# An empty step between the squares at a head's end and their column sums

## The chip, the cores and the metric

The kernel runs on one core of one Trainium2 chip. The metric is the device time of one execution in microseconds (us), and a version is told by the median of its runs. Before the change the median is 2241.21 us over three runs (2240.69 to 2246.49).

## The reference, cut to what matters

The reference is a two-layer trunk over 256 latent and 256 context tokens, 1024 channels wide, in float32. Each layer has three token mixers, merged by gates, and then a ConvFFN. Two of the mixers work in heads, eight each per layer, and both end a head with an RMS norm over its 128 channels:

```python
y_att = (rmsnorm(o, att_subln_g) * (1 - lam_init))      # differential attention
y_hg  = rmsnorm(o_f + flip(o_b), hg_norm_g) * silu(g)   # bidirectional HGRN2
rmsnorm(x, g) = x * rsqrt(mean(x * x, -1) + EPS) * g
```

The change moves nothing in the arithmetic. It concerns when, among other work, these two norms and all the steps ahead of them are issued. In layer 0 the heads produce all 512 tokens, in layer 1 the 256 latent ones only.

## The kernel before, in words

Layout. Activations lie with channels on the 128 partitions and tokens along the free axis. Each projection is three float32r matmul passes (high and low parts of weight and activation, `mm3`, lines 121 to 123); its weights come as float32 by DMA, ScalarE rounds them to the high part (line 111) and VectorE subtracts for the low part (line 112).

The heads stage. For each head h the kernel weaves three generators together: the projections that head h+1 needs (`project`, the main stream), the HGRN2 head h (`hg_head`) and the attention head h (`att_head`). `weave` (line 819) runs one step of the main stream, mostly 12 matmuls of 512 columns, then resumes the side generators up to their next `yield` where they are due. Side step i of c is due at `(i + 1) / (c + 1) * n * rate` main steps, where n is the number of main steps and c comes from the call:

```python
weave(main, n, m, (13, 2 * ns + 3), 0.92 if h + 1 < HEADS else (0.7, 0.85)[l])
```

So the counts are 13 for `hg_head`, and 11 (layer 0, ns = 4) or 7 (layer 1, ns = 2) for `att_head`. When the main stream has ended, what is left of the side generators runs to its end, `hg_head` first. A main stream has n = 12 steps in layer 0 and 9 in layer 1 where head h is even (below: a short head), and 8 more where h is odd (a long head: 20 and 17), because the values of two heads are projected at once. The last head of a layer is woven with `tail_proj` instead (n = 20 and 10, rates 0.7 and 0.85).

The order. TensorE's instructions stay in the order in which this Python code emits them. VectorE's, ScalarE's and GpSimd's are put in an order by a planner that works with its own costs: an instruction may be taken ahead of others that stand before it in the program, and work of head h+1 stands in VectorE's queue ahead of the end of head h. Each queue is then fixed and runs in order. PSUM has two sets of four banks: `pm` for the projections, `ps` for the heads.

The steps that this text speaks of, numbered by the `yield` that ends them:

- `hg_head`: H1 opens the head (gates, prefix sums, first level; no matmul). H2 sums the diagonal. H3 to H9 are six levels of masked products (matmuls at line 505, reading `K`, which VectorE makes in line 443 and GpSimd in line 445) with the neighbouring pairs among them. H10 makes the border products. H11 transposes the state keys (line 525) and ScalarE copies them out of PSUM (line 527). H12 multiplies them with the values (line 532), copied out in line 534. H13 accumulates the head's output `o` (lines 541 and 544) and takes the squares. What is behind the 13th `yield`, the column sums and the scaling, runs when the main stream has ended.
- `att_head`, layer 0 (layer 1): A1, A2 are the first scores (line 600); then transposes of the probabilities (line 617) and products with the values (line 624) alternate with further scores. A9 (A5) ends with the squares, A10 (A6) makes the column sums and scales, A11 (A7) is empty.

The norm itself: `rms_square` (line 312) has ScalarE square `o` (line 314) and round the squares to a high part (line 192), and VectorE make the low part (line 193); `rms_scale` (line 321) has TensorE sum both parts over the partitions with a matrix of ones (line 319), and ScalarE take the logarithm and the exponential (lines 325 and 326). The scaled head is stored to DRAM by SyncE's queue (line 942).

The scores of head h+1 need its queries and keys: `att_proj` ends each main stream of a short head with them, by a chain of VectorE (lines 575, 576, 581), GpSimd (line 577), ScalarE (line 582) and GpSimd again (line 583).

Of the kernel before, what the change touches and what calls it, by code (L numbers as in the profile page):

```python
# [21 lines left out]
HEADS = 8  # L22
# [25 lines left out]
def trunk(ctx: ExitStack, tc: tile.TileContext, A, out):  # L48
# [11 lines left out]
    @contextmanager  # L60
    def pool(name, side="left", **tags):
        with tc.tile_pool(name=name, bufs=1, side=side, reuse_waits="tile") as p:
            def get(tag, shape, dt=F32):
                return p.tile(shape, dt, tag=tag, name=tag, bufs=tags[tag])
            yield get
# [4 lines left out]
    def S(w):  # L70
        return sp.tile([P, w], F32, tag=f"s{w}", name=f"s{w}")
# [4 lines left out]
    def PS(shape):  # L76
        return psm.tile(shape, F32, tag="ps", name="ps")
# [22 lines left out]
    def pk(l, n):  # L100
        a, b = PK[n]
        return pack[l][:, a:b]
# [88 lines left out]
    def split(t, src):  # L191
        nc.scalar.copy(out=t[:, 0, :], in_=src)
        nc.vector.tensor_tensor(out=t[:, 1, :], in0=src, in1=t[:, 0, :].bitcast(F32), op=sub)  # L193
        return t
# [117 lines left out]
    def rms_square(get, o, n):  # L312
        sq = get("sq", [P, 512])
        nc.scalar.activation(out=sq[:, :n], in_=o, func=AF.Square)
        return sq, split(get("sqs", [P, 2, n], F32R), sq[:, :n])

    def column_sums(ps, parts):
        for i in range(2):
            nc.tensor.matmul(ps, lhsT=onesr, rhs=parts[:, 1 - i, :], start=(i == 0), stop=(i == 1))

    def rms_scale(sq, n):
        sq, parts = sq
        ms = PS([P, 512])
        column_sums(ms[:, :n], parts)
        nc.scalar.activation(out=sq[:, :n], in_=ms[:, :n], func=AF.Ln, scale=1.0 / P, bias=epsb)
        nc.scalar.activation(out=sq[:, :n], in_=sq[:, :n], func=AF.Exp, scale=-0.5)
        return sq
# [78 lines left out]
    def hg_head(get, l, h, z, k, q, gg, v, put, lbv, C0, NQ):  # L406
# [137 lines left out]
                    nc.tensor.matmul(o[:, c], lhsT=st[:, d, :], rhs=V[:, d, 0:T], start=False, stop=(d == 1))  # L544
        sq = rms_square(get, o, NQ)
        yield
        r = rms_scale(sq, NQ)
        nc.vector.scalar_tensor_tensor(out=r[:, :NQ], in0=o, scalar=pk(l, "hgn"), in1=r[:, :NQ], op0=mul, op1=mul)
        nc.vector.tensor_tensor(out=r[:, :NQ], in0=r[:, :NQ], in1=gg, op=mul)
# [36 lines left out]
    def att_head(get, l, qk, v, put, av, NQ):  # L586
        sc = 64 ** -0.5
        o = None

        def scores(qt):  # L590
            k0 = 0 if qt < 2 else 2
            nk = 4 - k0
            p = get("p", [P, 2, nk * P])
            mx = S(2)
            sm = S(2)
            pss = [PS([P, nk * P]) for _ in range(2)]
            for n, (a, b) in enumerate(((0, 1), (0, 0), (1, 0))):
                for i in range(2):
                    r = slice(64 * i, 64 * i + 64)
                    nc.tensor.matmul(pss[i], lhsT=qk[r, 0, a, qt * P:(qt + 1) * P], rhs=qk[r, 1, b, k0 * P:512],  # L600
                                     start=(n == 0), stop=(n == 2))
            for i in range(2):
                nc.vector.tensor_reduce(out=mx[:, i:i + 1], in_=pss[i], axis=AX.X, op=amax)  # L603
            nc.vector.tensor_scalar(out=mx, in0=mx, scalar1=-sc, scalar2=None, op0=mul)
            for i in range(2):
                nc.scalar.activation(out=p[:, i, :], in_=pss[i], func=AF.Exp, bias=mx[:, i:i + 1], scale=sc,
                                     accum_out=sm[:, i:i + 1])
            nc.vector.reciprocal(out=sm, in_=sm)
            nc.vector.tensor_tensor(out=sm[:, 1:2], in0=sm[:, 1:2], in1=av[:, 0:1], op=mul)
            nc.vector.tensor_scalar(out=p[:, 1, :], in0=p[:, 1, :], scalar1=sm[:, 1:2], scalar2=None, op0=mul)  # L610
            nc.vector.scalar_tensor_tensor(out=p[:, 0, :], in0=p[:, 0, :], scalar=sm[:, 0:1], in1=p[:, 1, :], op0=mul, op1=add)
            return p, k0, nk

        def turn(p, k0, nk):
            pt = PS([P, nk, P])
            for s in range(nk):
                nc.tensor.transpose(pt[:, s, :], p[:, 0, s * P:(s + 1) * P], ident)
            wt = get("wt", [P, nk, P])
            nc.scalar.copy(out=wt, in_=pt)
            return wt, k0, nk  # L620

        def values(qt, wt, k0, nk):
            for s in range(nk):
                nc.tensor.matmul(o[:, qt * P:(qt + 1) * P], lhsT=v[:, k0 + s, :], rhs=wt[:, s, :], start=(s == 0), stop=(s == nk - 1))

        n = NQ // P
        ps, ws = {}, {}
        for i in range(n + 2):
            if i < n:
                ps[i] = scores(i)  # L630
                yield
            if 2 <= i:
                if o is None:
                    o = PS([P, NQ])
                values(i - 2, *ws.pop(i - 2))
            if 1 <= i <= n:
                ws[i - 1] = turn(*ps.pop(i - 1))
                yield
        sq = rms_square(get, o, NQ)
        yield  # L640
        r = rms_scale(sq, NQ)
        nc.vector.scalar_tensor_tensor(out=r[:, :NQ], in0=o, scalar=av[:, 1:2], in1=r[:, :NQ], op0=mul, op1=mul)
        put(r[:, :NQ])
        yield
# [174 lines left out]
    def weave(main, n, sides, counts, rate):  # L819

        todo = sorted((((i + 1) / (c + 1) * n * rate, k) for k, c in enumerate(counts) for i in range(c)))
        done = 0
        end = object()
        while True:
            while todo and (todo[0][0] <= done or main is None):
                next(sides[todo.pop(0)[1]], None)
            if main is None:
                break
            if next(main, end) is end:
                main = None  # L830
            done += 1
        for g in sides:
            for _ in g:
                pass
# [100 lines left out]
    for l in range(DEPTH):  # L935
        ns = 4 if l == 0 else 2
# [4 lines left out]
        def putter(b, h):  # L941
            return lambda t: nc.sync.dma_start(out=ysp[b, h], in_=t)
# [23 lines left out]
        with pool("heads", lk=2, qg=1, qk=1, v=3, w=2, sq=2, sqs=2 if l else 1, wt=2, sc=1, E=6 if l else 4, K=2, p=2) as get, ExitStack() as even, \  # L966
                tc.issue_after(pre.ins):
            gete = even.enter_context(pool("even", lk=2, qg=1, qk=1, t=3, sh=2))
            gets = [lambda tag, *a: (gete if tag in ("lk", "qg", "qk", "t", "sh") else get)(tag, *a),
                    lambda tag, *a: (gete if tag in ("t", "sh") else get)(tag, *a)]  # L970

            def project(h, out, pss=None):
                if pss is not None:
                    yield from hg_proj(gets[h % 2], l, h, Xh, NQ, out, pss)
                if h % 2 == 0:
                    yield from v_proj(get, A["w_hi"][l, h // 2], Xh, out, "vh", whi if h == 0 else None)
                if pss is None:
                    yield from hg_proj(gets[h % 2], l, h, Xh, NQ, out)
                yield from att_proj(gets[h % 2], l, h, Xh, rope, NQ, out)
                if h % 2 == 0:  # L980
                    yield from v_proj(get, A["w_av"][l, h // 2], Xh, out, "va")

            def units(h):
                return (12 if l == 0 else 9) + (8 if h % 2 == 0 else 0)

            d = {}
            for _ in project(0, d, first):
                pass
            for h in range(HEADS):
                j = slice((h % 2) * P, (h % 2 + 1) * P)  # L990
                m = [hg_head(get, l, h, d["ls"], d["k"], d["qg"][:, 0, :], d["qg"][:, 1, :], d["vh"][:, :, j], putter(1, h),
                             lbv, (reset, masks), NQ),
                     att_head(get, l, d["qk"], d["va"][:, :, j], putter(0, h), attv[l], NQ)]
                if h + 1 < HEADS:
                    main, n = project(h + 1, d), units(h + 1)
                else:
                    even.close()
                    getv = rvt.enter_context(pool("vt", side="right", vt=ns))
                    vt = [getv("vt", [P, D]) for _ in range(ns)]
                    pus = []  # L1000
                    main, n = tail_proj(l, Xh, vt, ns, NQ, pus), 8 * ns // 2 + ns
                weave(main, n, m, (13, 2 * ns + 3), 0.92 if h + 1 < HEADS else (0.7, 0.85)[l])
        if l == 0:
            jobs += [(lambda get, scr, m=m: ada_row(get, scr, 0, m, 2)) for m in range(16, 48)]
        pre = nc.scalar.preload_act_table(AF.Gelu_apprx_tanh)
# [204 lines left out]
```

## Time and profile before

| | us |
|---|---|
| median of three runs | 2241.21 |
| the profiled execution | 2245.93 |
| its span, first to last instruction | 2244.2 |
| TensorE busy | 2128.5 (95%) |
| VectorE busy | 1727.2 (77%) |
| ScalarE busy | 1155.8 (52%) |

The span is what one profiled execution took from its first to its last instruction; the 1.7 us around it count in the time. A busy share is a mean over the whole kernel. The heads of layer 0 lie at about 90 to 660 us of the span, those of layer 1 at about 1450 to 1860 us. The profile names PE for TensorE, PEld for its weight loads, DVE for VectorE, ACT for ScalarE, POOL for GpSimd, SP for SyncE, and L319 for line 319; a tile stands without its buffer number.

### The profile page before, as it was taken

What the parts mean: (1) busy time and instruction counts of PE and PEld (TensorE: products, weight loads), DVE (VectorE), ACT (ScalarE), POOL (GpSimd) and SP (SyncE); (2) the same over time, 40 slices, a digit from 0 to 9 for tenths busy, and PEclk for the clock granted to TensorE, in tenths of its full rate; (3) what the DMA queues carried; (4) which work ended last, traced back from release to release, by engine and by line L of the source; (5) the groups of instructions that cost most, each with busy time, mean ns of one, the idle gap of its engine ahead of it and who ended that gap; (6) DMA issues with size and microseconds to landing.
All of it is one profiled execution on the core that took longest, in us unless ns stands there. A gap on an engine that the chain in (4) does not pass through costs nothing. (4 is left out here: it accounts for less than half of the span.)

```text
span 2244.2 us, 32759 instructions
## 1 busy us (share of the span) xinstructions
PE 2128.5 (95%) x12400; PEld 1849.0 (82%) x12400; DVE 1727.2 (77%) x2885; ACT 1155.8 (52%) x1913; POOL 324.7 (14%) x276
## 2 busy tenths in 40 slices
PE   6999999999999999998999998999999989997998
PEld 4878888788888877877887877988888879997997
DVE  7799897998857884448876776898998976567786
ACT  3666565665553222335442333666666655456664
POOL 4332132321300000002000001222221210001000
PEclk9999999999999999999999999999999999999999
DMA  7222222122245665344555653222232336554554
GB/s 257 101 71 71 76 76 66 66 71 71 66 149 185 224 201 94 100 141 154 161 179 184 195 144 127 99 91 89 84 96 81 98 98 211 196 192 141 185 195 138
DMA packets 93488, 293.21 MB, mean 131 GB/s; under 512 B 16017, under 2 KB 20753, under 8 KB 93073
## 3 DMA queue, kind: packets, MB, share of 16 engines
q1 hardware_dynamic: 93042, 290.59, 39.9%
q8 instruction: 98, 1.61, 0.3%
q14 instruction: 60, 0.49, 0.1%
q10 hardware_dynamic: 288, 0.52, 0.1%
HBM read 282.66 MB, written 8.41 MB: 130 GB/s over the span
## 5 line engine op out<-in xcount | busy, mean ns | idle before, releaser
L121 PE MATMUL pm<-X,wh 128*128 128x512 f32 (+1 forms) x2032 | 715.8, 352 | 18.2 <-POOL X L253 9.8
L123 PE MATMUL pm<-X,wl 128*128 128x512 f32 (+1 forms) x2032 | 699.0, 344 | 1.2 <-POOL wl L112 1.2
L122 PE MATMUL pm<-X,wh 128*128 128x512 f32 (+1 forms) x2032 | 698.8, 344 | 0.0
L112 DVE TENSOR_TENSOR wl<-wr,wh 128x1024 fp32r<-128x1024 f32 x398 | 492.9, 1243 | 192.6 <-ACT wh L111 187.8
L111 ACT CAST wh<-wr 128x1024 fp32r<-128x1024 f32 x408 | 422.2, 1039 | 313.0 <-PE pm L122 188.3
L121 PEld LDWEIGHTS pm<-X,wh 128*128 128x128 f32 x2032 | 386.5, 190 | 69.1 <-POOL X L253 11.9
L123 PEld LDWEIGHTS pm<-X,wl 128*128 128x128 f32 x2032 | 386.6, 190 | 49.8 <-POOL wl L112 2.7
L122 PEld LDWEIGHTS pm<-X,wh 128*128 128x128 f32 x2032 | 386.3, 190 | 42.1
L225 DVE SCALAR_TENSOR_TENSOR wj<-wa,scr 128x1024 f32<-128x1024 f32 x128 | 156.3, 1221 | 63.8 <-DMA wa<-in_ada_row 60.9
L445 POOL TENSOR_TENSOR K<-qg,E 128x512 f32<-128x512 f32 (+1 forms) x96 | 130.6, 1362 | 466.6 <-PE ps L505 313.6
L121 PE MATMUL pm<-wl,X 128*128 128x256 f32 (+1 forms) x608 | 187.3, 308 | 0.0
L123 PE MATMUL pm<-wh,X 128*128 128x256 f32 (+1 forms) x608 | 183.4, 302 | 0.0
L122 PE MATMUL pm<-wh,X 128*128 128x256 f32 (+1 forms) x608 | 183.2, 301 | 0.0
L202 POOL TENSOR_TENSOR s<-s,mhalf 128x1 f32<-128x1 f32 x26 | 14.4, 552 | 1077.1 <-DVE s L199 1037.1
L121 PE MATMUL pm<-ys,wh 128*128 128x512 f32 (+1 forms) x384 | 129.8, 338 | 8.8 <-ACT wh L111 5.1
L439 DVE TENSOR_TENSOR E<-lk 128x512 f32<-128x512 f32 (+1 forms) x192 | 124.3, 680 | 9.5 <-PE ps L544 8.2
L123 PE MATMUL pm<-ys,wl 128*128 128x512 f32 (+1 forms) x384 | 129.6, 338 | 0.0
L122 PE MATMUL pm<-ys,wh 128*128 128x512 f32 (+1 forms) x384 | 129.4, 337 | 0.0
L121 PEld LDWEIGHTS pm<-wl,X 128*128 128x128 f32 x608 | 117.0, 192 | 6.4 <-issue 2.2
L122 PEld LDWEIGHTS pm<-wh,X 128*128 128x128 f32 x608 | 116.8, 192 | 4.2
L123 PEld LDWEIGHTS pm<-wh,X 128*128 128x128 f32 x608 | 116.6, 192 | 4.3
L440 ACT ACTIVATE E<-E 128x1024 f32<-128x1024 f32 (+1 forms) x96 | 80.8, 846 | 62.7 <-DVE E L439 61.5
(247 smaller groups left out, 3551.8 us busy)
## 6 DMA issues: line engine op xcount, KB each, us to landing
wr<-in_w_up SPq DMA_DIRECT2D x88, 512.0 KB, 4.3
wa<-in_ada_row SPq DMA_DIRECT2D x80, 512.0 KB, 4.1
wr<-in_w_gate SPq DMA_DIRECT2D x48, 512.0 KB, 4.2
wr<-in_w_dn SPq DMA_DIRECT2D x40, 512.0 KB, 4.2
wr<-in_w_hqg SPq DMA_DIRECT2D x32, 512.0 KB, 3.7
wr<-in_w_hff SPq DMA_DIRECT2D x32, 512.0 KB, 3.6
wr<-in_w_aqk SPq DMA_DIRECT2D x32, 512.0 KB, 3.6
wr<-in_w_hi SPq DMA_DIRECT2D x16, 512.0 KB, 4.2
```

The costliest lines, as they stand in the source:

```text
L111: nc.scalar.copy(out=hi, in_=raw)
L112: eng.tensor_tensor(out=lo, in0=raw, in1=hi.bitcast(F32), op=sub)
L121: nc.tensor.matmul(ps, lhsT=lh, rhs=rl, start=first, stop=False)
L122: nc.tensor.matmul(ps, lhsT=lh, rhs=rh, start=False, stop=False)
L123: nc.tensor.matmul(ps, lhsT=ll, rhs=rh, start=False, stop=last)
L202: nc.gpsimd.tensor_tensor(out=r, in0=r, in1=mhalf, op=ALU.pow)
L225: nc.vector.scalar_tensor_tensor(out=junk, in0=raw, scalar=1.0, in1=scr[:, v, :], op0=mul, op1=mul, accum_out=mod[l][:, m, v:v + 1])
L439: nc.vector.tensor_tensor(out=dst, in0=ref if first else src, in1=src if first else ref, op=sub)
L440: nc.scalar.activation(out=E, in_=E, func=AF.Exp)
L445: nc.gpsimd.tensor_tensor(out=mkap(KQ[:], dims, NQ), in0=mkap(q, dims), in1=mkap(E[:], [[2 * b, np_], [b - NQ, 2], [1, b]], NQ), op=mul)
```

## The change

Both kinds of head get a second `yield` between the squares and the column sums, and the counts given to `weave` rise by one each, from (13, 2 * ns + 3) to (14, 2 * ns + 4). The new step does nothing. H14 and, in `att_head`, A10 (layer 1: A6) are now empty; the column sums of the attention head move to A11 (A7) and its empty last step to A12 (A8). As the divisor c + 1 grows from 14 to 15 and from 12 to 13 (layer 1: 8 to 9), every step of both heads falls due earlier. No instruction is added or removed.

```diff
@@ hg_head
         sq = rms_square(get, o, NQ)
         yield
+        yield
         r = rms_scale(sq, NQ)
@@ att_head
         sq = rms_square(get, o, NQ)
+        yield
         yield
         r = rms_scale(sq, NQ)
@@ the heads loop
-                weave(main, n, m, (13, 2 * ns + 3), 0.92 if h + 1 < HEADS else (0.7, 0.85)[l])
+                weave(main, n, m, (14, 2 * ns + 4), 0.92 if h + 1 < HEADS else (0.7, 0.85)[l])
```

## Rows read from the trace of the kernel before

**Rows 1.** The page, busy time of each engine, share, instructions.
```profile
PE 2128.5 (95%) x12400; PEld 1849.0 (82%) x12400; DVE 1727.2 (77%) x2885; ACT 1155.8 (52%) x1913; POOL 324.7 (14%) x276
```
**Rows 2.** Waits of TensorE, heads of layer 0: total us, times, longest.
```profile
PE ps L319 <- DVE sqs L193: 6.7, 6, 1.8
...
PE ps L600 <- ACT p L606: 0.3, 1, 0.3
```
**Rows 3.** Waits of TensorE, heads of layer 1.
```profile
PE ps L319 <- DVE sqs L193: 10.1, 7, 2.7
PE ps L617 <- DVE p L611: 4.2, 1, 4.2
PE ps L600 <- POOL qk L583: 2.6, 2, 1.8
```
**Rows 4.** Waits of TensorE in short head 2, layer 0, 249.09 to 306.7 us.
```profile
PE ps L624 <- DVE sc L463: 1.5, 1, 1.5
PE ps L319 <- DVE sqs L193: 1.0, 1, 1.0
PE ps L617 <- ACT p L606: 0.8, 1, 0.8
PE ps L600 <- POOL qk L583: 0.5, 1, 0.5
PE ps L505 <- DVE K L443: 0.3, 1, 0.3
```
**Rows 5.** Waits of TensorE in short head 4, layer 0, 384.4 to 443.7 us.
```profile
PE ps L319 <- DVE sqs L193: 2.7, 2, 1.8
...
```
**Rows 6.** Waits of VectorE, 249.09 to 304.8 us (short head 2, layer 0).
```profile
DVE sc L463 <- PE ps L505: 0.5, 1, 0.5
```
**Rows 7.** Waits of VectorE, 384.6 to 441.5 us (short head 4, layer 0).
```profile
DVE wl L112 <- ACT wh L111: 1.3, 1, 1.3
```
**Rows 8.** Waits of VectorE, 1574.5 to 1605.9 us (short head 2, layer 1).
```profile
DVE E L414 <- ACT E L412: 0.4, 1, 0.4
```
**Rows 9.** Timeline, column sums at heads' ends: start, us, what [idle before <-releaser].
```profile
164.86 0.73 PE L319 MATMUL ps<-sqs,onesr 128*128 128x512 f32 x2 [0.24 <-DVE sqs L193]
...
1556.56 0.50 PE L319 MATMUL ps<-sqs,onesr 128*128 128x256 f32 x2 [0.28 <-DVE sqs L193]
...
1763.67 0.51 PE L319 MATMUL ps<-sqs,onesr 128*128 128x256 f32 x2 [0.49 <-DVE sqs L193]
...
1805.03 0.77 PE L319 MATMUL ps<-sqs,onesr 128*128 128x256 f32 x2 [2.69 <-DVE sqs L193]
```
**Rows 10.** Timeline, transposed state keys on TensorE and their copies on ScalarE.
```profile
149.76 0.60 PE L525 MATMUL ps<-ident,E 128*128 128x128 f32 x4
151.60 0.58 ACT L527 COPY w<-ps 128x512 f32<-128x512 f32 x1
...
558.33 0.60 PE L525 MATMUL ps<-ident,E 128*128 128x128 f32 x4
559.37 0.58 ACT L527 COPY w<-ps 128x512 f32<-128x512 f32 x1
...
1842.29 0.60 PE L525 MATMUL ps<-ident,E 128*128 128x128 f32 x4
1843.39 0.59 ACT L527 COPY w<-ps 128x512 f32<-128x512 f32 x1
```
**Rows 11.** Timeline, VectorE early in short head 2 of layer 1.
```profile
1563.35 1.22 DVE L478 TENSOR_TENSOR E<-E,lk 128x1024 f32<-128x1024 f32 x1 [1.19 <-ACT E L477]
```
**Rows 12.** Timeline, keys ready on GpSimd and first scores on TensorE.
```profile
441.24 1.25 POOL L583 TENSOR_TENSOR qk<-t,qk 128x256 fp32r<-128x256 f32 x1 [2.35 <-ACT qk L582]
443.55 0.96 PE L600 MATMUL ps<-qk 64*128 64x512 f32 x6
...
1810.08 1.89 POOL L583 TENSOR_TENSOR qk<-t,qk 128x256 fp32r<-128x256 f32 x1 [2.60 <-ACT qk L582]
1812.42 0.96 PE L600 MATMUL ps<-qk 64*128 64x512 f32 x6
```

## The prediction

> **What bounds the kernel now.** I read the page first: TensorE is busy for 2128.5 us of the span, 95%, VectorE for 77% [rows 1]. By that mean the kernel is TensorE's, and what a change of order can win is TensorE's idle time. So I read next whom TensorE waits for in the two heads stages. The column sums (L319) wait for the low part of the squares (VectorE, L193) for 6.7 us in layer 0, six times, and 10.1 us in layer 1, seven times [rows 2, 3]. These 16.8 us, 0.75% of the time, are all that the change aims at, and no gain can be larger unless other waits fall with them.
>
> The third view is what VectorE waits for in the same stretches, and there the picture turns. In short head 2 of layer 0 VectorE waits once, 0.5 us, in 55.7 us [rows 6]; in the last 31 us of short head 2 of layer 1 its longest wait is 0.4 us [rows 8]. In a short head VectorE, not TensorE, is the engine that never rests: the 12 (9) projection steps are too few to cover one head's work on it. TensorE's waits there are the difference between two loads, and the reader is to see that they add up to the same sum wherever they fall. Short head 2: 1.5 + 1.0 + 0.8 + 0.5 + 0.3 = 4.1 us [rows 4]. Short head 4 has the sums' waits at 2.7 and none at the scores; with its other three as in head 2 that is 5.3, but VectorE itself lost 1.3 there [rows 7], and 5.3 - 1.3 = 4.0 us [rows 5, 7]. Where the sums waited longer, the scores at the next head's begin did not wait.
>
> This matters because of what stands behind the sums. The scores of the following long head need keys from a chain through VectorE and GpSimd. In two heads of layer 1 they are waited for already, 2.6 us together [rows 3], in head 2 of layer 0 for 0.5 us [rows 4]; where they are not, they came just in time: at 441.24 + 1.25 = 442.49 for scores at 443.55, 1.06 us ahead, and at 1811.97 for 1812.42, 0.45 us ahead [rows 12]. TensorE arriving earlier waits there instead.
>
> The Trainium skill (Perfetto Trace Analysis, Identifying the Most-Contended Engine) says that occupancy tells which engine to improve for VectorE, while TensorE's matmul occupancy is a bad measure, being pipelined. The trace agrees in that the engine at 77% is the one without gaps in a short head [rows 6, 8]. Read by TensorE's busy row alone the change would be worth up to 16.8 us, by the skill's rule next to nothing in short heads.
>
> **The change part by part.** No instruction is added, so only positions count. A side step i falls due at i / (c + 1) of n times the rate, rounded up to a main step; I worked this out for every head.
>
> (a) Short heads of layer 0 (n = 12, four of them). The attention squares move from step 9 to 8, their sums stay at 10: two steps between them instead of one. Their waits are the 6.7 us less the two at the heads' very ends, 0.24 [rows 9] and 2.7 - 1.8 = 0.9 [rows 5]: 5.6 us, gone. **-5.6.**
>
> (b) But H11 and H12 now fall due at the same main step 9 (before: 9 and 10). The product with the values then follows the transposes with no projections between them and waits for ScalarE's copy. From the transposes' end to the copy's end the trace has 151.60 + 0.58 - 149.76 - 0.60 = 1.82 us in the first and 1.02 in the last of the four [rows 10]; the other two are 1.85 and 1.05. Together **+5.7**. It is at least the copy itself, 0.58 each, 2.3 in all; at most I allow half as much again, 8.6, if ScalarE's queue is fuller at the new place. I take 5.7, which is the very pair of instructions.
>
> (c) Also in these heads H13 moves from step 11 to 10, so the sums at the end come two steps behind the squares: 0.24 + 0.9 [rows 5, 9], **-1.1**. It is within what the scores behind allow in head 4 (1.06 us [rows 12]).
>
> (d) Long heads of layer 0 (three, n = 20). The second scores A2 move from step 4 to 3 and stand right behind H2. That asks for `ps` banks which the first scores may still hold. The one place where this neighbourhood exists with a wait is the 0.3 us for the exponentials [rows 2]: 3 x 0.3, **+0.8**; between 0 and 0.9. The rest of these heads has no step that joins another closely.
>
> (e) Short heads of layer 1 (n = 9). Here H13 stays at step 8 and the sums stay at the end: one step between them as before. Of the 10.1 us, 9.0 are these (10.1 less 1.05 of the long heads, below) and the change does not touch them, though it puts H12 ahead of step 8. H11 and H12 join at step 7, with a wait of some 1.0 us each (as the 1.09 in (f) below), in a stretch where VectorE has no gaps; I cost that at nothing, because TensorE then waits less for the squares behind it; without that cover it is 4 x 1.0. What may gain: every attention step moves one main step earlier (A1 from step 2 to 1), and VectorE gets the first scores before its idle 1.19 us [rows 11], which is alike in heads 2, 4 and 6. The dense stretch then starts and ends that much earlier. For heads 2 and 4 I count it in full, **-2.4**; the bound is 0, if something else holds the first levels.
>
> (f) The last head of layer 1 (n = 10). Its A1 too moves from step 2 to 1. From the sums at 1805.03 to the scores at 1812.42 lie two steps [rows 9, 12], 3.4 us each less the sums' 0.5; the keys were ready only 0.45 us ahead. One step earlier TensorE waits 3.4 - 0.45 = 2.95; if head 6 ends 1.2 earlier as in (e), 1.75. This isn't given back at once: TensorE waits 4.2 us for probabilities a little later [rows 3], and has one step less to do before it gets there. H11 and H12 join here as well: 1843.39 + 0.59 - 1842.29 - 0.60 = 1.09, less 0.3 for the attention sums that stand between [rows 10], 0.8. Together **+2.6**, from 0 (the 4.2 us shrink by as much) to +3.8.
>
> (g) Long heads of layer 1 (n = 17). The squares move from step 15 to 14, the sums stay at the end: 0.28 twice and 0.49, the first and last of three [rows 9], **-1.05**; between that and 0.
>
> The sum is -5.6 + 5.7 - 1.1 + 0.8 - 2.4 + 2.6 - 1.05 = -1.05 us on the profiled execution's 2245.93, or 2244.9. That execution lies 4.7 above the median of the runs, 2241.21, so I predict **2240.2**: no change that can be told. With each term's friendlier end, (b) 3.4, (d) 0.8, (e) 1.2 for head 6 and (f) 2.6 less, it is 8.0 lower, 2232; with the other ends, (b) 2.9, (d) 0.1, (e) 2.4 and 4.0, (f) 1.2 and (g) 1.05 more, 11.7 higher, 2252.
>
> **The rivals.** *The waits go and stay gone.* VectorE's queue isn't fixed: a planner orders it, and in its order work for the next head stands ahead of the squares. If earlier squares also draw the chain for the keys forward, the dense stretches end earlier and the scores move with them. For it: VectorE rests in long heads, so work can be put off to them. Against it: the sums of waits in heads 2 and 4, equal within 0.1 us [rows 4, 5, 7]. Price: (a), (c) and (g) in full, (b) at its least, (e) -3.6, (f) 0, (d) 0: -5.6 - 1.1 - 1.05 + 2.3 - 3.6 = -9.05, 2232.
>
> *Slower: the steps bunch.* One mechanism: with divisors grown and the number of main steps not, more steps of `hg_head` share a main step, and the second of a pair needs what another engine makes from the first. H11 and H12 in nine heads, H3 and H4, H7 and H8 in the four short ones of layer 0. If VectorE's density doesn't cover these waits, they come on top: (e) 4.0 more without its gain of 2.4, (f) at 3.8, and at the levels one wait as the key products' 0.3 [rows 4] twice in four heads, 2.4, gives -1.05 + 6.4 + 1.2 + 2.4 = +9.0, 2250. It decides from some 6.7 + 1.05 = 7.8 us of new waits that nothing covers. For it: these copies are waited for by nobody now, so nothing in the trace shows them absorbed. Against it: they fall where VectorE is late anyway [rows 6, 8].
>
> *The change doesn't do what it says.* In the short heads of layer 1 it doesn't (e): the sums stay one step behind the squares; in the forecast already.
>
> **How the numbers follow.** About 0.3% (6.7 us) is what a measurement of this kernel can tell from no change. The forecast has 0.55 (0.47 of it within 6.7 us, 0.04 on each side), the first rival 0.2 (0.17 faster, 0.03 the same), the bunching 0.25 (0.2 slower, 0.05 the same). So faster 0.21, same 0.55, slower 0.24. The range reaches to the two rivals' times and the bounds, 2231 to 2252, which leaves out tails of about a tenth on either side.
>
> **What would show it.** (a), (c), (g): L319 waits for L193 no more in layer 0 and in long heads of layer 1, and still some 9 us, less the new copies' waits, in the short ones of layer 1. (b): L532 waits for L527, near 1.8, 1.0, 1.8, 1.0 us in layer 0. (e): VectorE's 1.19 us ahead of L478 are gone. (f): L600 waits for L583 by 2 to 3 us at the last head. The core of it: L600 behind short heads waits for L583 longer than before, where TensorE came earlier. I am wrong if TensorE's waits in the heads stages fall by over 7 us in sum, or if L532's waits are there and the other waits have not shrunk by as much.

## The result: 1.8% slower, and the profile after

The changed kernel takes 2281.1 us, median of four runs, against 2240.95 for the kernel before on the same chip: a ratio of 1.0178 [1.0159, 1.0197], 40 us slower. The forecast was no change, 2240.2 in a range of 2231 to 2252; it was wrong, and the time lies 29 us outside the range.

The profiled execution of after took 2280.97 us, its span 2279.1, 34.9 more than before. (Behind line 547 its line numbers are one higher, behind 641 two higher: L600 of before is L601.) The page's busy row, beside [rows 1]:

```profile
PE 2139.4 (94%) x12400; PEld 1854.9 (81%) x12400; DVE 1747.1 (77%) x2885; ACT 1156.1 (51%) x1913; POOL 309.9 (14%) x276
```

The instructions are the same in number; TensorE's busy time grew by 10.9 us and its gaps by more. Whom TensorE waits for in the heads of layer 0 (90 to 680 us; total, times, longest), beside [rows 2]:

```profile
PE ps L505 <- DVE sc L463: 12.1, 6, 2.9
PE ps L505 <- DVE s L605: 6.6, 4, 2.0
PE ps L532 <- ACT w L527: 5.1, 4, 1.8
PE ps L525 <- DVE E L517: 4.8, 3, 1.6
...
PE ps L601 <- POOL qk L584: 1.3, 4, 0.3
...
```

and in layer 1 (1450 to 1900 us), beside [rows 3]:

```profile
PE ps L601 <- ACT p L607: 10.4, 10, 2.7
PE ps L319 <- DVE sqs L193: 8.1, 4, 2.0
PE ps L532 <- ACT w L527: 5.4, 5, 1.1
PE ps L601 <- POOL qk L584: 3.4, 2, 3.1
...
PE ps L618 <- DVE p L612: 1.4, 1, 1.4
```

The waits that the change aims at are gone from layer 0: L319 stands in the first view no more. In their place stand waits of L505, the masked products, for VectorE's L463 and L605, 18.7 us, of which the same view of before has no row. With the four rows left out (4.0, 3.4, 1.4 and 0.3) the first view adds up to 39.0 us, and the same view of before to 19.3: 19.7 us more. The last column sums of layer 0 end 22.8 us later. In layer 1 the six largest rows add up to 30.3 us (1.6 of it left out here), those of before to 22.5.

Where the time went by heads is read from the column sums that end each head. In after (start, us, what), beside [rows 9]:

```profile
310.72 0.68 PE L319 MATMUL ps<-sqs,onesr 128*128 128x512 f32 x2
392.36 0.63 PE L319 MATMUL ps<-sqs,onesr 128*128 128x512 f32 x2
...
1578.89 0.41 PE L319 MATMUL ps<-sqs,onesr 128*128 128x256 f32 x2
1626.23 0.51 PE L319 MATMUL ps<-sqs,onesr 128*128 128x256 f32 x2 [2.02 <-DVE sqs L193]
```

Long head 3 of layer 0 lasts 81.6 us from end to end (392.99 less 311.40), before 76.8; the three long heads of layer 0 grew by 5.3, 4.8 and 5.3. Short head 2 of layer 1 lasts 47.4 (1626.74 less 1579.30), before 41.3; heads 4 and 6 grew from 41.3 and 41.6 to 46.0 each. The first head of layer 0 ended 3.2 us later, the other short heads there grew by 0.5 to 2.5 each, and long heads of layer 1 became 0.7 to 2.5 us shorter.

### The profile page after: what moved, and what is told of

It reads as the page before. It is cut to its first block, busy times and chain, and to the rows that moved or that the text cites. A ratio compares the mean times of both kernels' runs of the same rounds, so it can differ in the third digit from the quotient of the medians.

```text
span 2279.1 us, 32745 instructions
## 1 busy us (share of the span) xinstructions
PE 2139.4 (94%) x12400; PEld 1854.9 (81%) x12400; DVE 1747.1 (77%) x2885; ACT 1156.1 (51%) x1913; POOL 309.9 (14%) x276
## 5 line engine op out<-in xcount | busy, mean ns | idle before, releaser
L112 DVE TENSOR_TENSOR wl<-wr,wh 128x1024 fp32r<-128x1024 f32 x398 | 499.2, 1259 | 221.0 <-ACT wh L111 215.3
L439 DVE TENSOR_TENSOR E<-lk 128x512 f32<-128x512 f32 (+1 forms) x192 | 125.4, 684 | 1.2
L440 ACT ACTIVATE E<-E 128x1024 f32<-128x1024 f32 (+1 forms) x96 | 81.1, 846 | 76.2 <-DVE E L439 74.0
```

Of the source, the lines that this page charges most:

```text
L112: eng.tensor_tensor(out=lo, in0=raw, in1=hi.bitcast(F32), op=sub)
L439: nc.vector.tensor_tensor(out=dst, in0=ref if first else src, in1=src if first else ref, op=sub)
L440: nc.scalar.activation(out=E, in_=E, func=AF.Exp)
```

## The experiments

**Which part carries the loss: the empty step, or the earlier dues?** The change does two things. The first run keeps both `yield`s and gives every old step its old due, so that what is behind the new step comes one due later:

```diff
-        todo = sorted((... for k, c in enumerate(counts) for i in range(c)))
+        todo = sorted((... for k, c in enumerate(counts) for i in range(c + 1)))
-                weave(main, n, m, (14, 2 * ns + 4), ...
+                weave(main, n, m, (13, 2 * ns + 3), ...
```

> Both empty steps are in, but every older step falls due where it did before the change (weave lists one step more with the old divisor, so the empty step of the HGRN2 head is due last and the attention sums one due later). Theory 1 (the loss is the earlier dues of all the other steps, which bring scores and level products together until the four ps banks are full): no loss, 2234 to 2243 us, ratio to before 0.997 to 1.001, L505 and L600 wait for banks no more than before (under 4 us in the heads of layer 0). Theory 2 (the loss is the step itself, which keeps the heads' outputs and squares longer in PSUM and SBUF): slow like the changed kernel, 2270 to 2285.

The second is the kernel before, with the divisors of the change and no new step:

```diff
-        todo = sorted((((i + 1) / (c + 1) * n * rate, k) ...
+        todo = sorted((((i + 1) / (c + 2) * n * rate, k) ...
```

> No empty step; the divisor of the dues is one larger (c + 2 for c + 1), so every step falls due where the changed kernel puts it, and the attention sums follow the squares one due behind. Theory 1: slow like the changed kernel, 2270 to 2290 us, with the waits of L505 on L463 (some 12 us in layer 0) and of the second scores on the exponentials (some 2.7 us in each short head of layer 1). Theory 2: as before the change, 2235 to 2248.

Measured: the new step alone 2250.05, 1.0043 [1.0018, 1.0068], where no loss was expected; the dues alone 2281.52, 1.0186 [1.0169, 1.0203], all of the loss. TensorE's waits in layer 0 with the dues alone are in the main those of after; the first row:

```profile
PE ps L505 <- DVE sc L463: 12.0, 6, 2.9
...
```

The new step alone costs too, by another way. In its layer 0 TensorE waits for the squares 17.9 us, four times. One of these, on the timeline:

```profile
304.09 0.58 ACT L314 ACTIVATE sq<-ps 128x512 f32<-128x512 f32 x1
304.84 0.74 DVE L644 SCALAR_TENSOR_TENSOR sq<-ps,attv,sq 128x512 f32<-128x512 f32 x1
...
307.33 0.68 DVE L193 TENSOR_TENSOR sqs<-sq,sqs 128x512 fp32r<-128x512 f32 x1
308.16 1.00 PE L319 MATMUL ps<-sqs,onesr 128*128 128x512 f32 x2 [4.18 <-DVE sqs L193]
```

The attention head's logarithm, exponential (L325 and L326, from 302.47) and scaling (L644), one due later, stand on ScalarE and VectorE ahead of the squares of `hg_head` (L314, L193). Work of the next head stands between them (L440 on ScalarE, and L439 on VectorE, 1.91 us from 305.50), and the sums at the head's end wait 4.18 us.

**Which of the two heads?** Each change alone, with its own count:

```diff
+        yield                       (hg_head only)
-                weave(main, n, m, (13, 2 * ns + 3), ...
+                weave(main, n, m, (14, 2 * ns + 3), ...
```

> The step and the count in the HGRN2 heads only (14, 2 ns + 3). Theory 1: a part of the loss, the one that comes from H11 beside H12 and from levels that share a main step: nine waits of some 1.1 us on the copied keys and a few us at the levels, 2248 to 2262 us; no wait of the second scores on exponentials in layer 1. Theory 2: little, 2240 to 2250, since this output was already held to the end of the head.

```diff
+        yield                       (att_head only)
-                weave(main, n, m, (13, 2 * ns + 3), ...
+                weave(main, n, m, (13, 2 * ns + 4), ...
```

> The step and the count in the attention heads only (13, 2 ns + 4). Theory 1: the second scores of short heads in layer 1 fall due behind H2 and H3 and wait for banks, 2.7 us four times and a slower clock behind them, so 2252 to 2270 us; no waits on the copied keys (L532). Theory 2: nearly all of the loss, 2270 to 2285, since it is the attention output that is now held a step longer beside the HGRN2 steps.

`hg_head` alone 2250.7, 1.0051 [1.0035, 1.0068]; `att_head` alone 2276.65, 1.016 [1.0134, 1.0187]. The larger part comes with the attention's steps. The 2276.65 lies in the range that was named for the other theory, heads' outputs held longer; but the dues alone have no new step, and all of the loss.

By layers the two parts do not add up (one profiled execution each, by the last column sums of each layer's heads). With `hg_head` alone those of layer 0 end 8.6 us later than before, with `att_head` alone 26.4, with both 22.8. From there to the end of layer 1's heads it takes 1.0 us less, 0.2 more, and with both 11.2 more: layer 1 loses only by the two together.

**Which heads of the eight?** Both parts for even h alone, and for odd h alone:

```diff
+        if h % 2 == 0:
+            yield                   (both places; counts likewise)
```

> The whole change, but only where h is even (short heads); the others as before. By the spans from head end to head end the short heads of the changed kernel lost some 7 us in layer 0 and 19 in layer 1, so 2260 to 2268 us if heads add up. If VectorE's backlog is handed from head to head and the sum over two heads is what counts (the view behind the prediction), it is nearer to before, 2245 to 2255.

```diff
+        if h % 2 == 1:
+            yield                   (both places; counts likewise)
```

> The whole change, but only where h is odd (long heads and the last). By the spans between head ends the long heads of layer 0 lost 15 us and those of layer 1 won 4, so 2247 to 2253 us if heads add up, with three waits of L505 and L525 in each long head of layer 0. The prediction had these heads at +0.8, by which it would be 2238 to 2242.

Short heads alone 2257.43, 1.0088 [1.0073, 1.0103], a little less than expected; long heads alone 2263.05, 1.0109 [1.0091, 1.0127], 10 us more than the range expected. The two add up to 1.97%, near the 1.78% of both: heads lose by themselves, and neither kind gives back what the other lost. For the long heads and the last the forecast had +2.35 us, by (d), (f) and (g).

**Do the masked products wait for PSUM banks?** L463 and L605 read the scores and products out of `ps`; a bank comes free behind them. In the changed kernel, the attention's output `o` of layer 0 goes to a bank of `pm`, and as a control the same in the kernel before:

```diff
-                    o = PS([P, NQ])
+                    o = PB([P, NQ])
```

> The changed kernel with one edit: the attention head's output o is put in a bank of pm instead of one of the four of ps, so that scores, levels and transposes have all four. Bank theory (the new waits of TensorE are for free ps banks): the waits of L505 on L463 and on the maximum (18.7 us in layer 0 in the changed kernel) and of the second scores on the exponentials (10.7 us in layer 1) fall to under a third, 2248 to 2262 us. Rival (the levels' products K come late, since VectorE gets two levels' work at once, and the bank is free anyway): those waits stay under other names, 2272 to 2285. Should pm be short with three banks for the projections, waits of L121 to L123 for VectorE and ScalarE appear in the heads.

> The kernel before with the same edit: o of the attention head in a pm bank. Bank theory: the old dues hardly ever fill the four banks, so little happens, 2230 to 2243 us (the waits of L624 and L617 on merges, 4.6 us and less, may go). If three pm banks are too few it is slower, above 2246.

After with the bank: 2272.99, 1.0147 [1.0125, 1.0169]; the control 2237.45, 1.0009 [0.999, 1.0029]. The 18.7 us of L505 behind L463 and L605 are gone and short heads of layer 0 are back at 58 to 59 us: these were waits for banks. The gain is 0.31% all the same, less than the bank theory expected. In short heads L618 waits 3.8 us for the same L463 and the sums 7.1 for the squares. The long ones stay at 80.6 to 82.1, with the products' wait for ScalarE's copy,

```profile
PE pm L625 <- ACT wt L620: 7.0, 3, 2.3
```

once in each, and with a lower granted clock, 0.98, 0.96 and 0.98 over the three heads, where after has 1.00 over long head 3. In layer 1, where the waits were to fall too, nothing moved (L601 behind L607 11.3 us), because `o` is allocated later there than the second scores. The banks that matter in layer 1 are those of H2's sums and the first level, which stand between the two scores:

```diff
-        pl = PS([P, NS, 2, P])
+        pl = (PB if l else PS)([P, NS, 2, P])
-            pl = PS([P, NQB, P])
+            pl = (PB if l and n == 0 else PS)([P, NQB, P])
```

> The changed kernel; in layer 1 the diagonal sums of H2 and the first level of H3 use a pm bank, so that two ps banks are free when the second scores come (the first scores hold the other two). Putting o into pm could not help there, since o is taken later. Bank theory for layer 1: the scores' wait on the exponentials (10.7 us) falls below 3 us and the drop of the clock behind it with it, short heads of layer 1 fall from 46 to 47 us towards 42 to 43, 2262 to 2272 us. Rival (VectorE is late with the maxima and everything behind them whatever the banks): the wait moves to the next instructions, 2276 to 2284.

2272.06, 1.0156 [1.0137, 1.0176]. L601's waits for L607 are gone from layer 1, so they too were for banks; but as much comes back in waits of L618 for what is next, L612, L463 and L607 (14.7 us in sum; L618 waited 1.4 us in after):

```profile
PE ps L618 <- DVE p L612: 8.2, 3, 2.7
...
PE ps L618 <- DVE sc L463: 3.9, 1, 3.9
```

**Are the copied keys' waits covered?** In the changed kernel H12 falls due three quarters of a step later in short heads and in the last one of layer 1, so that projections stand between it and H11:

```diff
-        todo = sorted((((i + 1) / (c + 1) * n * rate, k) ...
+        todo = sorted((((i + 1 + 0.75 * (n < 13 and k == 0 and i == 11)) / (c + 1) * n * rate, k) ...
```

> The changed kernel, with H12 due 0.75 of a step later in main streams of under 13 steps, so that it no longer shares a main step with H11. L532's waits on the copied keys (10.5 us, nine times) should be gone. If they cost what they show, 2268 to 2273 us; if VectorE's backlog covers them, as the prediction had it for layer 1, other waits grow and it stays at 2277 to 2284.

2266.74, 1.0139 [1.0118, 1.0159]. L532's 10.5 us are gone; in layer 1 L544 now waits 8.1 us for the copy in line 534. It is 0.4% less than after, so the waits at L532 were not covered.

**Is VectorE too late, whatever the banks?** If TensorE merely asks earlier than VectorE can answer, the change must cost less once VectorE has less to do. Both kernels with the low part of the weights (L112) left out for the projections of gates, queries, keys and values; the high part stands in its place in the products, so TensorE's work is the same and the output is not the reference's:

```diff
+        if not low:
+            return [(hi[:, i, :], hi[:, i, :]) for i in range(k1 - k0)]
...                                 (low=False where these weights are loaded)
```

> The kernel before, with less work for VectorE in the heads stages: the low part of the projections' weights there is left out (L112 for hff, hqg, aqk, hi, av; the third matmul pass runs with the high part in its place, so TensorE does as many matmuls and the values are not the reference's). VectorE loses 7.4 us of work in a short head and 12.4 in a long one. TensorE's waits of 40 us in the heads should fall; 2205 to 2232 us.

> The changed kernel with the same lighter VectorE (the same part of the computation left out). If the loss of 40 us is VectorE being late for steps that fall due earlier, most of it goes: within 12 us of the lightened kernel before. Rival (the steps that share a main step wait for each other's latencies and for banks whatever VectorE's load): still 25 us or more above it.

Before: 2226.89, 0.9955 [0.9938, 0.9972]. After: 2240.75, 1.0009 [0.9992, 1.0027]. With the lighter VectorE the change costs 13.9 us by the medians, 0.54% by the ratios in place of 1.78%: nearer to the 12 us at most of the first expectation than to the rival's 25 at least. Long head 3 of layer 0 takes 76.6 us with the change and 75.7 without. In all of it (305.3 to 381.9 us) one wait of TensorE is left, and VectorE is busy for 53.18 of 76.60 us (the waits and the window of after with the lighter VectorE, whose line numbers are two higher than those of after):

```profile
PE ps L527 <- DVE E L519: 0.3, 1, 0.3
```

```profile
305.30:381.90 76.60, 76.17 (x485) 66.81 (x485) 53.18 (x98) 45.01 (x79) 15.34 (x14) 1.00 0.20 72
```

So some two thirds of the loss go with VectorE's load: it is late for steps that fall due earlier. Leaving L112 out also frees a step of the chain that brings the weights, and the planner makes a new order for VectorE; how much of the 26 us is either was not separated.

The short heads of layer 0 are another case. There the masked products still wait for banks, 13.7 us in four heads where after has 10.7, in three of them for the exponentials that still read the scores:

```profile
PE ps L507 <- ACT p L609: 10.6, 3, 3.6
```

**Do the cures add up?** The two moves of banks and the later H12 together, as in the diffs above:

> The changed kernel with the edits of e5, e8 and e11 together (attention output and, in layer 1, the diagonal sums and the first level in pm banks; H12 apart from H11). Alone they won about 0.3, 0.2 and 0.4% over the changed kernel. If they are separate parts of the loss, 2258 to 2264 us, 0.8 to 1.1% above before, and the rest is VectorE's lateness. If each wait only moves to the next place, 2266 to 2280.

2257.29, 1.0076 [1.0049, 1.0103]. The single gains against after (0.31, 0.22 and 0.39%) would give 1.0086. They add up, and 0.8% remain that no bank and no later H12 takes away.

**A version that beats both.** The first run made the short heads of layer 1 shorter (39.2 to 39.9 us) and those of layer 0 longer. So the empty step in layer 1 alone, every old step at its old due:

```diff
+        if l:
+            yield                   (both places)
-        todo = sorted((... for k, c in enumerate(counts) for i in range(c)))
+        todo = sorted((... for k, c in enumerate(counts) for i in range(c + extra)))
-                weave(main, n, m, (13, 2 * ns + 3), 0.92 if ... )
+                weave(main, n, m, (13, 2 * ns + 3), 0.92 if ... , l)
```

> The empty steps in layer 1 alone, with the old dues (layer 0 as before the change). In e1_step_old_dues the heads of layer 1 took some 5 to 7 us less than before and those of layer 0 some 16 more. If these are separate effects, 2229 to 2237 us, faster than before by 0.2 to 0.4%. If the shorter heads of layer 1 were a matter of that run's clock alone, 2238 to 2243.

2235.26, 0.9982 [0.9968, 0.9996], 3 to 4 us faster than before, by an interval that just leaves out 1. In layer 1 TensorE's wait for the squares fell from 10.1 us, seven times [rows 3], to

```profile
PE ps L319 <- DVE sqs L193: 4.6, 3, 1.5
```

## Why the prediction was wrong

**The step that failed: term (d), +0.8 us where the three heads measured +15.4, and behind it "VectorE rests in long heads".** The forecast read VectorE's waits in two stretches of short heads; for long heads it shows no row. Their mean bears the claim out, and the windows of long head 3 show what it hides. Before (stretch, its us, busy time and count of PE, PEld, DVE, ACT and POOL, granted clock, DMA share, GB/s), the head, its middle and its end:

```profile
300.40:377.20 76.80, 75.97 (x485) 67.27 (x485) 63.40 (x108) 45.66 (x80) 21.91 (x17) 1.00 0.21 69
...
320.00:362.00 42.00, 41.64 (x233) 35.30 (x232) 40.82 (x71) 25.79 (x45) 12.32 (x8) 1.00 0.16 53
362.00:377.20 15.20, 15.20 (x117) 14.80 (x116) 7.22 (x13) 8.05 (x13) 2.73 (x3) 1.00 0.27 87
```

after, the middle and the end:

```profile
330.00:373.00 43.00, 38.32 (x215) 31.76 (x213) 40.99 (x67) 24.76 (x43) 10.38 (x7) 1.00 0.19 63
373.00:393.00 20.00, 20.00 (x139) 18.81 (x138) 10.77 (x17) 9.76 (x15) 4.05 (x4) 1.00 0.21 66
```

Over the head VectorE is busy for 63.40 of 76.80 us, 83%; in the middle for 40.82 of 42.00, 97%, and TensorE is full as well. The middle is as tight as a short head. Steps due one main step earlier there can only wait: TensorE's busy time in it falls from 41.64 of 42 to 38.32 of 43 us. And nothing gives it back, for at the head's end TensorE has no idle time (20.00 of 20.00, before 15.20 of 15.20), while VectorE is busy for 10.77 of 20.00. In the whole head (300.4 to 377.2 us) before had

```profile
PE ps L600 <- POOL qk L583: 0.5, 1, 0.5
...
```

0.9 us of waits, so there was nothing for a new wait to take the place of; after (311.4 to 393.0 us) has

```profile
PE ps L525 <- DVE E L517: 1.6, 1, 1.6
PE ps L505 <- DVE s L605: 1.5, 1, 1.5
PE ps L505 <- DVE sc L463: 1.1, 1, 1.1
...
```

and 0.7 us in two smaller ones: 4.9 us, 4.0 more, of the 4.8 by which the head grew. The two waits of L505 on the timeline (the rows between left out):

```profile
345.31 0.62 PE L601 MATMUL ps<-qk 64*128 64x256 f32 x6
346.21 0.72 DVE L463 COPY_PREDICATED sc<-masks,ps 128x512 f32<-128x512 uint8 x1
347.07 1.13 PE L505 MATMUL ps<-K 128*128 128x128 f32 x8 [1.15 <-DVE sc L463]
...
351.60 0.71 DVE L463 COPY_PREDICATED sc<-masks,ps 128x512 f32<-128x512 uint8 x1
352.20 0.15 DVE L605 TENSOR_SCALAR s<-s 128x2 f32<-128x2 f32 x1
352.45 1.13 PE L505 MATMUL ps<-K 128*128 128x128 f32 x8 [1.51 <-DVE s L605]
```

Each masked product starts right behind the end of VectorE's read that frees its bank; the scores ahead of it took two banks, and `o` holds another. Before, the same two steps stand the other way round, the product first:

```profile
336.98 1.05 PE L505 MATMUL ps<-K 128*128 128x128 f32 x8
337.96 0.62 PE L600 MATMUL ps<-qk 64*128 64x256 f32 x6
```

By the formula of the dues these scores, A6, and the product, H7, fall due together before, at 6/12 and 7/14, and `hg_head` goes first; with the grown divisors 6/13 lies ahead of 7/15. All ten waits of L505 behind L463 and L605 in layer 0 stand at H7 or H8 behind the scores of A6: 8.0 us in long heads, and 10.7 in short ones, where H8 too now follows A6 in the same main step:

```profile
281.88 1.58 PE L505 MATMUL ps<-K 128*128 128x128 f32 x8 [2.88 <-DVE sc L463]
```

With `hg_head` alone these waits are 1.5 us, with `att_head` alone there are none. The claim "The rest of these heads has no step that joins another closely" looked for new pairs. It did not look for pairs that turn round, and counted banks for A2 behind H2 alone. That wait, the one that (d) had priced, did not come: these scores start at 321.91 us with no idle time ahead of them.

**The first step's premise, that waits in a dense stretch add up to the same sum, fails in (e).** In the short heads of layer 1, costed at -2.4 us, VectorE's 1.19 us of idle ahead of L478 [rows 11] did go, as foreseen. But the first scores take two banks, H2's sums and the first level one each, and the second scores want two more than the four there are. That is so before as well. There ScalarE has copied H2's sums (L487) and VectorE has read the first level (L463) by the time the second scores come, so two banks are free:

```profile
1562.59 0.96 PE L600 MATMUL ps<-qk 64*128 64x512 f32 x6
...
1565.03 0.36 ACT L487 COPY sc<-ps 128x256 f32<-128x256 f32 x1
...
1565.69 0.43 DVE L463 COPY_PREDICATED sc<-masks,ps 128x256 f32<-128x256 uint8 x1
...
1567.16 0.96 PE L600 MATMUL ps<-qk 64*128 64x512 f32 x6
```

After, short head 2:

```profile
1582.02 0.96 PE L601 MATMUL ps<-qk 64*128 64x512 f32 x6
...
1586.04 0.61 PE L505 MATMUL ps<-K 128*128 128x128 f32 x4
1586.63 1.23 DVE L478 TENSOR_TENSOR E<-E,lk 128x1024 f32<-128x1024 f32 x1
...
1587.78 0.69 DVE L605 TENSOR_SCALAR s<-s 128x2 f32<-128x2 f32 x1
1588.50 0.69 ACT L607 ACTIVATE p<-ps,s 128x512 f32<-128x512 f32 x1 [1.42 <-DVE s L605]
...
1589.33 0.49 PE L601 MATMUL ps<-qk 64*128 64x512 f32 x1 [2.68 <-ACT p L607]
...
1595.58 0.63 PE L121 MATMUL pm<-X,wh 128*128 128x512 f32 x1
1596.01 0.63 PE L122 MATMUL pm<-X,wh 128*128 128x512 f32 x1
```

The second scores are wanted as far behind the first as before, 3.7 us behind their end (1586.65 less 1582.98; before 3.6). But the first scores came a main step earlier, while VectorE was still at other work; it takes their maxima (L604) from 1585.36 only, and L478 then stands ahead of L605. So ScalarE's exponential L607 starts 5.5 us behind the scores' end, before 2.7, and L487 and L463 come behind it (1589.84 and 1590.26). The bank that L607 reads from 1588.50 to 1589.19 is the first to come free, and the second scores take it then. TensorE, in order, waits 2.68 us ahead of a step of projections that nothing held, and L505 behind these comes late for VectorE, whose longest wait in the head (1579 to 1626 us) is now

```profile
DVE sc L463 <- PE ps L505: 2.9, 1, 2.9
```

That is the point at which the premise ends: it holds while VectorE never stops. An early step can make the full engine itself wait, and then the time is lost to both. Heads 2, 4 and 6 of layer 1 grew by 4.3 to 6.1 us each; 2 and 4 were to shrink by 1.2. With `att_head` alone, where the order of these steps is the same, the waits here are 1.0 us and heads 2, 4 and 6 take 41.1, 42.6 and 41.1 us.

The premise had a weak reading behind it too. The view of [rows 6] begins with a line that stands neither there nor in the prediction's "VectorE waits once, 0.5 us":

```profile
DVE s L608 <- ACT p L606: 1.5, 1, 1.5
```

Head 4 has the same line beside the 1.3 us of [rows 7]. With all of VectorE's waits taken off, the sums that were to be equal within 0.1 us are 4.1 - 2.0 = 2.1 and 5.3 - 2.8 = 2.5; the prediction took off 1.3 in head 4 and nothing in head 2.

**Terms that held.** (a), (c) and (g): L319's waits are gone from layer 0 and from long heads of layer 1. The short heads of layer 0 grew all the same, by the bank waits of L505 above, for which no term stood. (b): L532 waits 5.1 us in layer 0, four times, longest 1.8, against 5.7 forecast, by the very pair of instructions. In layer 1 the same pair, costed at nothing under VectorE's cover in short heads, waits 5.4 us, five times, and the later H12 showed these waits to be real. (f): the last head's scores wait 3.1 us for L584, but L618's 4.2 [rows 3] fell to 1.4, and the head got no longer (48.9 us, then 48.6): the term's lower bound, 0. The sign that was named as the core, longer waits of the scores for L583 behind short heads, did not show: 1.2 us in layer 0 before and 1.3 after, and in layer 1, apart from the last head's 3.1, 2.6 before and 0.2 after.

**The rivals.** The bunching had the sign and the right doubt ("nothing in the trace shows them absorbed"), and its pairs at L532 wait as it said. It also named H7 and H8 in the four short heads of layer 0, at the price of a key product's 0.3 us; H8 waits 2.1 us in the first and 2.9 in each of the others, for a bank. Its price of +9 was too small by 31: banks, and VectorE late for all that is due earlier, weren't in it. The Trainium skill (Perfetto Trace Analysis, Identifying the Most-Contended Engine) has the engine with the highest occupancy go first, and for TensorE goes by its weight loads. Over the whole kernel that is TensorE (82% against VectorE's 77% [rows 1]); in the middle of a long head it is VectorE, with 40.82 of 42.00 us against 35.30. The runs agree there, in that the change cost a third with a lighter VectorE.

What stays open: of the 0.54% that remain with the lighter VectorE only the bank waits in short heads were placed, and the 0.8% that remain with all three cures were not taken apart. The planner can put VectorE's queue in another order in every run (L478 stands ahead of the first scores' maxima before, at 1563.35, and behind them after, at 1586.63), and no run held its order fixed.

## What to carry to other kernels

When steps are spaced by a divisor, one more step moves them all: look for steps whose dues tied and now turn round, and list for every new neighbourhood which buffers it holds at once, and not only which pair shares a slot. Read density in stretches of a few steps inside one iteration, since a mean of 83% can hide a middle of 97% in which an earlier request is a wait. A missing step between a producer and its consumer is better put in where it is missing, with every other due left as it is.

## What the runs showed of the hardware

A wait in the middle of the heads can cost more than itself. In the 6.8 us behind the 2.68 us wait of (e) the granted clock is 0.50, which is the 1.2 GHz level:

```profile
1589.70:1596.50 6.80, 6.62 (x18) 4.69 (x18) 4.27 (x10) 1.67 (x5) 0.00 (x0) 0.50 0.00 0
```

The projections there start 0.43 us apart (1595.58 and 1596.01 above), and ahead of the wait, at a granted clock of 1.00, 0.23 (1585.35 and 1585.58). Over twelve of them that is 2.4 us, nearly the wait once more.

Not every such wait had this behind it. Behind the like waits of heads 4 and 6, 2.67 and 2.66 us, the clock is 0.50 from 1699.0 to 1702.3 and from 1804.8 to 1808.1 us, about half as long; behind the 1.01 us with `att_head` alone it is 1.00 (1589.0 to 1592.9). The kernel before has waits as long at the sums of heads 2, 4 and 6: behind the 2.59 us of the first the clock is 1.00 (1598.4 to 1605.0), behind the 2.71 and 2.69 of the others 0.50 (from 1702.5 and 1804.9, for 3.3 us and more).

Over the heads of layer 1 the granted clock fell from 0.9826 of 392.9 us to 0.9706 of 406.8. As an estimate, span times what is missing to 1, 6.8 and 12.0 us were lost: some 5 of the 13.9 by which the stretch grew.
